# Output projection of an encoder layer: sixteen plain blocks, or one level of Strassen's form under a list scheduler

## The chip, the cores and the metric

The kernel runs on one core of a Trainium2 chip. The core has five engines that run side by side, each in the order of its own queue, and wait for one another through semaphores: PE (TensorE, matmuls into PSUM), DVE (VectorE), ACT (ScalarE), POOL (GpSimd) and SP (SyncE). DMAs are issued from SP's queue and from POOL's. The metric is the device time of one execution in microseconds (us). Three runs of the kernel before gave 1225.41, 1226.53 and 1227.11, median 1226.53.

## The reference

One encoder layer for 1024 tokens (`S`) of width 1024 (`D`), in float32:

```python
h = rmsnorm(x, norm1_g) * (1.0 + sc1) + sh1          # sh, sc, gt: from silu(c) @ w_ada + b_ada
z = h @ w_in                                         # u, v, q, k, va, gate_a, gate_b
a_out = gmlp_branch(u, v, gm_v_g, gm_w_s, gm_b_s) @ w_a
b_out = window_attention_branch(q, k, va, q_norm_g, k_norm_g, attn_sink) @ w_b
merged = jax.nn.sigmoid(gate_a) * a_out + jax.nn.sigmoid(gate_b) * b_out
x = x + gt1 * (merged @ w_o)                         # the output projection
h2 = rmsnorm(x, norm2_g) * (1.0 + sc2) + sh2
f_gate, f_up = jnp.split(h2 @ w_ffn_in, 2, axis=-1)
x = x + gt2 * ((jax.nn.silu(f_gate) * f_up) @ w_ffn_out)
```

The change concerns `merged @ w_o`, a product of 1024 x 1024 by 1024 x 1024, with the residual, the factor `gt1` and the sums of squares for the second norm.

## The kernel before, in words

Activations lie transposed: features on the 128 partitions, tokens along the free axis, in two token halves A and B of 512 (`HALF`). A float32 operand is split into a high part (rounded to fp32r, a cast on ACT) and a low part (the difference, a subtraction on DVE); a product is three matmuls, high by high, high by low and low by high (`mm3`, L161; `multiply`, L1286, for Strassen blocks). One matmul has a 128 x 128 stationary block and 512 moving columns. Nearly all operations are recorded under L79, the line of a small wrapper that can pin instructions to program order (`in_order`); loads are L131, stores L134.

The layer runs in this order.

- `half(0)` and `half(1)` (L568): for each token half the norm, the q and k projections, attention and gMLP. Attention is a loop of eight steps (four blocks of 128 tokens, two key/value heads; the `for s in range(nw)` loop). A step forms scores on PE, adds the bias and takes the maximum on DVE, takes exponentials on ACT (`exps`, which begins with a tiny DVE addition into `es`), normalises on DVE (`normalise`: sum, reciprocal, four products on the tiles `lb`), and in the next step transposes the tiles on PE. `fill` puts other matmuls (the u projection, two gate blocks) between. After the last step the transposes follow after two `fill` groups. Weight units are loaded by SP into a ring of three `raw` tiles, cast by ACT, and their low part in this loop is made by POOL.
- `ada_late` is one column block of the adaLN modulation: a DVE dot product of a 128 x 1024 weight tile with silu(c). 24 such blocks are worked off in the queue `ada_queue`: 4 at the end of `half(0)`, 12 in `half(1)`, and 8 in the output projection of half A, for which `cond` (silu(c)) is loaded again.
- `gate_products` (L1295): six of the eight 128-feature groups of the gates, already in one level of Strassen's form (Winograd's variant): the two token halves and the two halves of the contraction make 2 x 2 blocks, and seven products (`STEPS`) replace eight. Its results are the tiles `merged[half]`.
- `out_projection(hf, m, m_next)` (L1395), once for each half: for each of eight output groups `d`, eight contraction blocks of three matmuls (24 matmuls) into one PSUM bank, then on DVE `x1 = bank * gt1 + x`, the square on ACT and its addition on DVE, and a store of the rows to DRAM (`x1d`) on POOL's queue. A weight unit of w_o (128 x 1024) is prepared two groups ahead, so w_o is read twice. During half A the high and low parts of half B's `merged` are made, and the eight adaLN blocks. During half B the second norm of half A runs (`second_norm`, reading `x1d` back), and six units of the FFN's weights are made or loaded (`first_unit`, `early`, `raw2`). The order is that of the framework's scheduler, apart from the places that are pinned.
- The FFN, under `manual_schedule` (every engine's instructions in the order in which the code issues them): the first product pair of the gate, with `col_rstd` (column sums of half B's squares on PE) after the second product and `spread` (the reciprocal root, spread over partitions by PE) after the third; then seven products for each feature group, and the output product in the same form.

Tiles live in rings: `mid` has 8 tiles of 128 x 2048, `h` 4, `raw`, `wh` and `wl` (weights and their parts) 3 each, the PSUM banks `mm` and `at` 4 each. A new tile of a ring waits until an earlier one has been used for the last time.

Of the kernel before, what the change touches and what calls it, by code (L numbers as in the profile page):

```python
# [37 lines left out]
BIAS = 4  # L38


@with_exitstack
def kernel(
# [86 lines left out]

    def load(dst, src):  # L130
        tc.keep_in_program_order(nc.sync.dma_start(dst, src))  # L131
# [116 lines left out]
    tB = dram.tile([NP, P, 4 * HALF], F32, tag="tB", name="tB")  # L248

# [252 lines left out]
    def open_ffn():  # L502

        apool_ctx.close()
        fp = ffn_ctx.enter_context(pool("ffn"))
        fps.append(fp)
        for part in range(2):
            t = fp.tile([P, 2048], F32R, tag=f"b22{'hl'[part]}", name=nm("first"))
            firsts[part] = t

    def first_unit(i):

        r = raw_unit(w_gate[EARLY - 2 + i])
        h, l = (firsts[p][:, i * UNIT : (i + 1) * UNIT] for p in range(2))
        A.copy(h, r)
        V.tensor_tensor(l, r, h.bitcast(F32), op=ALU.subtract)
        return h, l
# [50 lines left out]
    def half(hf):  # L568
# [417 lines left out]
        pts = None  # L986
        for s in range(nw):
            if s:
# [3 lines left out]
                den = exps(*sc, work[s][1])  # L992
            fill(FA)
# [301 lines left out]
    def gate_products(hH, hL):  # L1295
# [21 lines left out]
        for d in GD:  # L1317
            banks = {}
            for i, (u, part, t, b, first) in enumerate(STEPS):
# [30 lines left out]
                elif i == 6:  # L1350
# [3 lines left out]
                    if d == KT - 1:  # L1354
                        split(merged[0][1][:, 3, :], mH[1][:, 3, :], mL[1][:, 3, :])
                    gate_low(d + 1, 1)
                run_tokens((0, 4, 4, 4, 0, 0, 0)[i])
                if d == KT - 1:
# [6 lines left out]
                    if i == 4:  # L1365
                        wo_units.append(unit(w_o[0]))
                    if i == 6:
                        wo_units.append(unit(w_o[1]))
# [21 lines left out]
        in_order[0] = False  # L1390
        return (mH, mL), merged[1]

    wo_units = []

    def out_projection(hf, m, m_next):  # L1395

        mH, mL = m
        if hf == 1:
            h2[0] = [[hid(), hid()], [hid(), hid()]]
            dst = h2[0]  # L1400
            x1B.extend([midt(F32, 4), midt(F32, 4)])
            h2m.extend([midt(F32, 4), midt(F32, 4)])
        else:
            out = [[midt(F32R, 4), midt(F32R, 4)] for _ in range(2)]
            cond = midt(F32, 2)[:, 0, :]
            load(cond, cd)
        ss = ss_tile()[:, :HALF]

        def second_norm(k):
            xk = stream("hs")  # L1410
# [4 lines left out]
        for d in range(KT):  # L1415
# [8 lines left out]
            if hf == 1 and d == 6:  # L1424
                early.append(unit(w_gate[0], V))
# [573 lines left out]
```

## Time and profile before

| | us |
|---|---|
| median of three runs | 1226.53 |
| span of the profiled execution | 1224.2 |
| PE busy | 1217.5 |
| PE weight loads busy | 1016.0 |
| DVE busy | 897.4 |
| ACT busy | 578.5 |
| POOL busy | 148.7 |

The profiled execution's own span, from its first instruction to its last, is 1224.2 us, 2.3 below the median of the runs, which also hold what lies around the span. An engine's busy time is the union of its instructions' records; matmul records overlap their successors, so the time of one matmul is read from start to start. A row of a timeline gives the start, the time from the first start to the last end, the engine, the line, the operation, the tile written and those read, and how many instructions are merged; in brackets stands the idle time before it and what ended it. The mean granted clock of PE was 1.000.

### The profile page before, as it was taken

Reading aid. Unit: us, or ns where it says so; the run is one execution under the profiler, and the core shown is the slowest. Engines: PE = TensorE matmul, PEld = TensorE weight load, DVE = VectorE, ACT = ScalarE, POOL = GpSimd, SP = SyncE. Lnnn points to the kernel's source line nnn. Section 1 sums busy time; section 2 is a strip of 40 time slices with the busy share of each in tenths; the row PEclk is TensorE's granted clock in tenths of the full one; section 3 lists DMA queues with packets and bytes.
Section 4 is the critical chain, followed back from the end, with each engine's and each line's share of the span. In section 5 each row is a group of like instructions: output and inputs, shape, how many; then the busy total and the mean of one; then the engine's idle time right before and its main releaser. Section 6 shows DMA issues by size and latency. Waiting matters only on the chain.

```text
span 1224.2 us, 15630 instructions
## 1 busy us (share of the span) xinstructions
PE 1217.5 (99%) x5701; PEld 1016.0 (83%) x5701; DVE 897.4 (73%) x1449; ACT 578.5 (47%) x944; POOL 148.7 (12%) x178
## 2 busy tenths in 40 slices
PE   9999999999999999999999999999999999999998
PEld 7888888888888888888888888888888888888887
DVE  9988877788878766877797766675676766765646
ACT  5667855367855434634453233333333334433341
POOL 0124323114331000011000001000000000010001
PEclk9999999999999999999999999999999999999999
DMA  9721179521176333597413446455555439995552
GB/s 366 283 86 52 35 241 361 223 86 53 35 276 222 120 104 121 198 322 264 154 52 120 172 155 224 172 176 202 189 189 187 167 153 367 393 364 190 189 172 104
DMA packets 75937, 230.79 MB, mean 189 GB/s; under 512 B 8658, under 2 KB 8914, under 8 KB 71124
## 3 DMA queue, kind: packets, MB, share of 16 engines
q1 hardware_dynamic: 61444, 161.62, 38.3%
q0 software_dynamic: 14416, 68.17, 14.9%
q8 instruction: 45, 0.74, 0.3%
q14 instruction: 32, 0.26, 0.1%
HBM read 174.70 MB, written 55.05 MB: 188 GB/s over the span
## 4 chain that ended last, share of the span: by engine, by line
PE 92%; DMA 4%; DVE 2%; issue 1%; ACT 1%; SPq 0%; POOL 0%; POOLq 0%; DVEq 0%; ACTq 0%
PE mm L79 48%; PE at L79 45%; DMA wS<-wo 1%; DMA mid<-in_w_ada_dram 1%; DMA raw<-in_w_q_dram 1%; DMA wo<-in_w_out_dram 1%; DMA mid<-in_xA_dram 0%; DVE mid L79 0%; ACT mid L79 0%; DVE wl L79 0%; DVE ws L79 0%; ACT wh L79 0%; DVE lb L79 0%; DVE hid L79 0%; DVE wo L79 0%
## 5 line engine op out<-in xcount | busy, mean ns | idle before, releaser
L79 PE MATMUL mm<-mid,wh 128*128 128x512 f32 x704 | 217.4, 390 | 0.0
L79 ACT CAST wh<-raw 128x1024 fp32r<-128x1024 f32 (+1 forms) x151 | 154.3, 1023 | 120.9 <-PE mm L79 45.6
L79 DVE TENSOR_TENSOR wl<-raw,wh 128x1024 fp32r<-128x1024 f32 (+1 forms) x137 | 161.5, 1183 | 62.1 <-ACT wh L79 61.1
L79 PEld LDWEIGHTS mm<-mid,wh 128*128 128x128 f32 x704 | 131.7, 188 | 27.1
L79 PE MATMUL mm<-mid,wl 128*128 128x512 f32 x352 | 137.0, 389 | 0.0
L79 PE MATMUL mm<-wh,h 128*128 128x512 f32 x384 | 124.6, 396 | 0.2 <-ACT h L79 0.2
L79 PE MATMUL mm<-h,wh 128*128 128x512 f32 x400 | 123.9, 391 | 0.0
L79 PEld LDWEIGHTS mm<-h,wh 128*128 128x128 f32 x400 | 74.6, 188 | 15.4
L79 PE MATMUL at<-h,wh 128*128 128x512 f32 x272 | 84.0, 390 | 0.0
L79 PEld LDWEIGHTS mm<-wh,h 128*128 128x128 f32 x384 | 70.8, 188 | 13.8 <-ACT h L79 0.4
L79 DVE TENSOR_TENSOR wl<-ws,wh 128x1024 fp32r<-128x1024 f32 (+1 forms) x54 | 60.7, 1125 | 24.5 <-ACT wh L79 24.5
L79 PE MATMUL mm<-h,wl 128*128 128x512 f32 x200 | 77.9, 389 | 0.0
L79 PEld LDWEIGHTS mm<-mid,wl 128*128 128x128 f32 x352 | 66.1, 188 | 13.8
L79 ACT CAST wh<-ws 128x1024 fp32r<-128x1024 f32 (+1 forms) x54 | 52.5, 973 | 42.3 <-DVE ws L79 27.4
L79 PE MATMUL mm<-wl,h 128*128 128x512 f32 x192 | 71.2, 391 | 0.0
L79 ACT ACTIVATE t<-t 128x512 f32<-128x512 f32 x53 | 32.8, 630 | 72.0 <-DVE t L79 71.9
L79 PEld LDWEIGHTS at<-h,wh 128*128 128x128 f32 x272 | 50.9, 188 | 10.5
L79 DVE TENSOR_TENSOR ol<-raw,oh 128x1024 fp32r<-128x1024 f32 x30 | 36.5, 1223 | 30.0 <-ACT oh L79 28.4
L79 ACT ACTIVATE xs<-xs 128x512 f32<-128x512 f32 x21 | 13.3, 633 | 94.0 <-DVE xs L79 94.0
L79 PE MATMUL at<-h,wl 128*128 128x512 f32 x136 | 53.1, 390 | 0.3 <-DVE wl L79 0.3
L79 PE MATMUL at<-wl,wh 128*128 128x512 f32 (+1 forms) x136 | 52.7, 388 | 0.0
L79 PE MATMUL at<-wh 128*128 128x512 f32 (+1 forms) x136 | 52.7, 387 | 0.0
(275 smaller groups left out, 2729.5 us busy)
## 6 DMA issues: line engine op xcount, KB each, us to landing
raw<-in_w_gate_dram SPq DMA_DIRECT2D x28, 512.0 KB, 3.8
tA<-hid POOLq DMA_DIRECT2D x11, 1024.0 KB, 4.6
tB<-hid POOLq DMA_DIRECT2D x11, 1024.0 KB, 5.0
wo<-in_w_out_dram POOLq DMA_DIRECT2D x22, 512.0 KB, 5.9
wS<-wo POOLq DMA_DIRECT2D x11, 1024.0 KB, 5.2
raw<-wS SPq DMA_DIRECT2D x44, 256.0 KB, 3.5
raw<-tB SPq DMA_DIRECT2D x44, 256.0 KB, 4.8
mid<-in_w_ada_dram SPq DMA_DIRECT2D x20, 512.0 KB, 9.8
```

Of the source, the lines that this page charges most:

```text
L79: ins = f(*args, **kw)
```

## The change

The output projection of both halves becomes one call, `out_products(merged)`, under `manual_schedule`. With A and B the token halves and the two halves of the contraction as blocks, four pairs of output groups (`p`, an even and an odd group) each take seven products of twelve matmuls: M1 and M2 for the even group of half A; T2, T3 and T4 accumulate onto M1's bank; T1 and B22 share another bank. 28 products take the place of sixteen groups of 24 matmuls, 336 matmuls of 384.

- The blocks T1 to T4 are sums of the `merged` tiles. The first sum (half A minus half B) is made for four tiles in `gate_products`, the others in `blocks()`, all on DVE, with the high part on ACT and the low part on DVE.
- Sums of w_o's blocks come out of `merged_sums`: in the attention loop of `half(1)` SP loads two units of w_o in every second step, DVE makes four sums, and POOL stores them to a new DRAM tensor `sO`, from which the projection loads them. The instructions stand between `exps` and `normalise`; the last step has four sums.
- The eight adaLN blocks move to the attention loop of `half(0)`, at the same place, one for each step from the second on and two in the last. The load of `cond` in the projection goes.
- Each product's bank is read by one DVE accumulation straight into the residual rows, scaled by `gt1` or its negative: 28 instead of 16. The even rows of half A are stored after M2 and loaded again for the norm; the other rows of x are loaded into tiles that the blocks have freed (`new_rows`). The second norm of half A is made in place on these rows after the product T1 of the second pair.
- The order of all of it, on PE, DVE, ACT, POOL and SP, comes from `Plan`: every operation is added with an engine, a cost and names that it reads and writes; PE's and SP's operations keep the order in which they were added; the others are picked by a simulated start and, among those that could start within 0.3 us, by the latest start that their users allow.
- The tiles of the FFN's first weights and of its T2 and B22 blocks change places (`tt2`, `b22`), and `unit(w_o[2])` is made one product earlier in `gate_products` in the place of `w_o[1]`.

The diff, cut:

```diff
+class Plan:
+    COST = {"v512": 0.6, "v1024": 1.14, "p512": 0.66, "a512": 0.52, "a1024": 0.95, "small": 0.2,
+            "load": 0.4, "mm": 2.72, "few": 0.45, "pow": 1.5}
+    WAIT = {"V": 0.08, "A": 0.08, "T": 0.4, "D": 3.4, "G": 0.1}
+    def __init__(self):
+        self.ops, self.last, self.users = [], {}, {}
+    def add(self, eng, cost, fn, reads=(), writes=()):
+        n = len(self.ops)
+        deps = set()
+        for r in reads:
+            if r in self.last:
+                deps.add(self.last[r])
+        for w in writes:
+            deps.update(self.users.get(w, ()))
+            if w in self.last:
+                deps.add(self.last[w])
+        for r in reads:
+            self.users.setdefault(r, []).append(n)
+        for w in writes:
+            self.last[w], self.users[w] = n, []
+        self.ops.append((eng, self.COST[cost], fn, deps))
+    def order(self, free):
+        n = len(self.ops)
+        late = [1e9] * n
+        t = 0.0
+        for i, (eng, cost, _, _) in enumerate(self.ops):
+            if eng == "T":
+                late[i] = t
+                t += cost
+        for i in reversed(range(n)):
+            eng, cost, _, deps = self.ops[i]
+            for j in deps:
+                e, c = self.ops[j][:2]
+                late[j] = min(late[j], late[i] - c - self.WAIT[e])
+        queues = {e: [i for i in range(n) if self.ops[i][0] == e] for e in "VATDG"}
+        now = {e: free.get(e, 0.0) for e in queues}
+        done, start = {}, {}
+        while len(start) < n:
+            best = None
+            for e, q in queues.items():
+                for i in q[:1] if e in "TD" else q:
+                    deps = self.ops[i][3]
+                    if all(j in done for j in deps):
+                        at = max([now[e]] + [done[j] for j in deps])
+                        key = (max(at, now[e] + 0.3), late[i], i)
+                        if best is None or key < best[0]:
+                            best = (key, e, i, at)
+            _, e, i, at = best
+            queues[e].remove(i)
+            start[i] = at
+            now[e] = at + self.ops[i][1]
+            done[i] = now[e] + self.WAIT[e]
+        return sorted(range(n), key=lambda i: (start[i], i))
+    def run(self, free):
+        for i in self.order(free):
+            if self.ops[i][2] is not None:
+                self.ops[i][2]()
...
+    def merged_sums(p):
+        t = mid.tile([P, 2048], F32, tag="mid", name=nm("wo"))
+        for i in range(2):
+            load(t[:, i * UNIT : (i + 1) * UNIT], w_o[2 * p + i])
+        a11, a12, a21, a22 = (t[:, i * HALF : (i + 1) * HALF] for i in range(4))
+        ops = [(a22, a21, a22), (a21, a11, a21), (a11, a22, a11), (a12, a11, a12)]
+        def one(n):
+            out, a, b = ops[n]
+            V.tensor_tensor(out, a, b, op=ALU.add)
+            if n == 3:
+                store(sO[p], t)
+        return one
...
+            if hf == 0:
+                if s % 2 == 0:
+                    ada_load()
+                if s:
+                    ada_late(*ada_loaded.pop(0), silu_c)
+                if s == nw - 1:
+                    ada_late(*ada_loaded.pop(0), silu_c)
+            else:
+                if s % 2 == 0:
+                    pair_sums.append(merged_sums(s // 2))
+                if s:
+                    for n in range(2):
+                        pair_sums[(s - 1) // 2](2 * ((s - 1) % 2) + n)
+                if s == nw - 1:
+                    for n in range(2):
+                        pair_sums[-1](2 + n)
...
+                if d in (4, 5) and i in (1, 3):
+                    k = 2 * (d - 4) + i // 2
+                    o = merged[1][0][:, k, :]
+                    V.tensor_tensor(o, merged[0][0][:, k, :], o, op=ALU.subtract)
...
+                    if i == 5:
+                        wo_units.append(unit(w_o[2]))
...
-    def out_projection(hf, m, m_next):
...
+    def out_products(merged):
+        (m0, m1), (x0, x1) = merged
+        NPAIR = KT // 2
+        T1 = oblk["T1"]
+        T2 = oblk["T2"] = (fpt("tt2h"), fpt("tt2l"))
+        B22 = oblk["B22"] = (fpt("b22h"), fpt("b22l"))
+        T3 = oblk["T3"] = (midt(F32R, 4), midt(F32R, 4))
+        T4 = oblk["T4"] = (midt(F32R, 4), midt(F32R, 4))
...
+        def blocks():
+            high("B21", m1, "m1", 3)
+            lo("B21", m1, "m1", 3)
+            for k in KS:
+                high("T1", x0, "x0", k)
+                lo("T1", x0, "x0", k)
+            for k in KS:
+                add("V", "v512", lambda k=k: negsum(x0[:, k, :], x1[:, k, :], x0[:, k, :]),
+                    [f"x1{k}"], [f"x0{k}"])
+                high("T2", x0, "x0", k)
+                lo("T2", x0, "x0", k)
+            for m, mn, name in ((m0, "m0", "T3"), (m1, "m1", "T4")):
+                for k in KS:
+                    add("V", "v512", lambda k=k, m=m: negsum(m[:, k, :], x0[:, k, :], m[:, k, :]),
+                        [f"x0{k}"], [f"{mn}{k}"])
+                    high(name, m, mn, k)
+                    lo(name, m, mn, k)
+            for k in KS:
+                high("B22", x1, "x1", k)
+                lo("B22", x1, "x1", k)
...
+        def fetch(key, parts):
+            r = f"raw{count['raw'] % 3}"
+            count["raw"] += 1
+            def go():
+                tiles[key] = wpool.tile([P, UNIT], F32, tag="raw", name=nm("raw"))
+                for cs, src in parts:
+                    load(tiles[key][:, cs], src)
+            add("D", "load", go, [], [r])
+            return r
+        def make(key, parts, to=None):
+            r = fetch(key, parts)
+            w = to
+            if to is None:
+                w = f"w{count['w'] % 3}"
+                count["w"] += 1
+            def hi():
+                if key not in units:
+                    units[key] = wtiles()
+                A.copy(units[key][0], tiles[key])
+            add("A", "a1024", hi, [r], [w + "h"])
+            add("V", "v1024", lambda: split_low(tiles[key], *units[key]), [r, w + "h"], [w + "l"])
+            names[key] = w
...
+        def need(kind, p):
+            if kind == "0":
+                make((kind, p), [(all_, w_o[2 * p])])
+            elif kind == "B":
+                make((kind, p), [(cs, w_o[2 * (p + i) + 1][:, HALF:]) for i, cs in enumerate((lo_, hi_))])
+            else:
+                i = "AC".index(kind)
+                make((kind, p), [(cs, sO[p][:, (2 * j + i) * HALF : (2 * j + i + 1) * HALF])
+                                 for j, cs in enumerate((lo_, hi_))])
...
+        USE = {"M1": ("0", 0, "B11", "a", True), "M2": ("0", 1, "B21", "b", True),
+               "T2": ("A", 0, "T2", "a", False), "T3": ("A", 1, "T3", "a", False),
+               "T4": ("B", None, "T4", "a", False), "T1": ("C", 1, "T1", "c", True),
+               "B22": ("C", 0, "B22", "c", False)}
...
+        def accumulate(get, tn, p, b, sc, d):
+            def go():
+                t = get()
+                V.scalar_tensor_tensor(out=t, in0=banks[p, b], scalar=sc[:, d : d + 1], in1=t,
+                                       op0=ALU.mult, op1=ALU.add)
+            add("V", "p512", go, [f"{'b' if b == 'b' else 'a'}{p}"], [tn])
...
+        need("0", 2)
+        c11 = [stream(("xs", "hs")[p % 2]) for p in range(NPAIR)]
+        for p in range(NPAIR):
+            add("D", "load", lambda p=p: load(c11[p], x_rows(0, 2 * p)), [], [f"c{p}"])
...
+        def new_rows(hf, q, old):
+            def go():
+                if hf == 0 and q == 0:
+                    h2[0] = [[hid(), hid()], [hid(), hid()]]
+                (x1B if hf else h2m).append(midt(F32, 4))
+            add("D", "load", go, [], [f"{old}{k}" for k in KS] + [f"{'gh'[hf]}{d}" for d in range(4 * q, 4 * q + 4)])
+            for d in range(4 * q, 4 * q + 4):
+                if hf or d % 2:
+                    add("D", "load", lambda d=d: load(row(hf, d), x_rows(hf, d)), [], [rn(hf, d)])
+        def even_rows(q):
+            for d in (4 * q, 4 * q + 2):
+                add("D", "load", lambda d=d: load(row(0, d), x1d[d * P : (d + 1) * P, :HALF]),
+                    [f"x1d0{d}"], [rn(0, d)])
...
+        new_rows(1, 0, "x0")
+        new_rows(0, 0, "m0")
...
+        second = [(p, name) for q in (0, 2) for name in ("T2", "T3", "T4") for p in (q, q + 1)]
+        for n, (p, name) in enumerate(second):
+            product(p, name)
+            if n == 2:
+                need("A", 2)
+            elif n == 3:
+                need("A", 3)
+                new_rows(1, 1, "m1")
+            elif n == 5:
+                need("B", 2)
+                new_rows(0, 1, "x1")
+            elif n == 7:
+                add("D", "load", new_firsts, [], [f"T2{x}{k}" for x in "hl" for k in KS]
+                    + [f"f{i}{x}" for x in "hl" for i in range(2)])
+                make(("f", 0), [(all_, w_gate[EARLY - 2])], "f0")
+            elif n == 8:
+                even_rows(0)
+                need("C", 0)
+            elif n == 9:
+                make(("f", 1), [(all_, w_gate[EARLY - 1])], "f1")
+                need("C", 1)
+                even_rows(1)
+            elif n == 11:
+                need("C", 2)
+            d = 2 * p + (name != "T2")
+            hf = int(name != "T4")
+            accumulate(lambda hf=hf, d=d: row(hf, d), rn(hf, d), p, "a", gt if name == "T2" else ngt, d)
+            if name == "T4":
+                square(lambda d=d: row(0, d), rn(0, d), 0, d)
...
+        third = [(p, name) for q in (0, 2) for name in ("T1", "B22") for p in (q, q + 1)]
+        for n, (p, name) in enumerate(third):
+            product(p, name)
+            if n == 0:
+                add("T", "few", col_sums, ["ss"], ["pt"])
+                add("V", "small", root_ms, ["pt"], ["ms"])
+                add("G", "pow", root, ["ms"], ["rcol"])
+            elif n == 1:
+                add("T", "few", spread_out, ["rcol"], ["rb"])
+                for k in range(KT):
+                    add("V", "p512", lambda k=k: norm_scale(k), ["rb"], [rn(0, k)])
+                    add("A", "a512", lambda k=k: norm_high(k), [rn(0, k)], [f"hh{k}"])
+                    add("V", "v512", lambda k=k: norm_low(k), [rn(0, k), f"hh{k}"], [f"hl{k}"])
+            elif n == 2:
+                need("C", 3)
+            elif n == 3:
+                make(("g", 0), [(all_, w_gate[0])])
+            elif n == 6:
+                make(("g", 1), [(all_, w_gate[1])])
+                fetch(("g", 2), [(all_, w_gate[2])])
+            d = 2 * p + (name == "T1")
+            accumulate(lambda d=d: row(1, d), rn(1, d), p, "c", ngt if name == "T1" else gt, d)
+            square(lambda d=d: row(1, d), rn(1, d), 1, d)
...
+        plan.run({"V": 2.5, "A": 1.5, "T": 0.0})
...
+    merged = gate_products(*half(1))
+    in_order[0] = False
+    manual[0] = True
+    with tc.manual_schedule():
+        out_products(merged)
...
```

198 lines of the change are left out of this document (119 added, 79 removed).

## The prediction

> **What bounds the kernel now.** I read the page first (busy shares, then the chain that ended last), then a table of stages, then the timelines of PE, DVE and POOL around the stages that the diff touches.
>
> ```profile
> span 1224.2 us, 15630 instructions
> PE 1217.5 (99%) x5701; PEld 1016.0 (83%) x5701; DVE 897.4 (73%) x1449; ACT 578.5 (47%) x944; POOL 148.7 (12%) x178
> PE 92%; DMA 4%; DVE 2%; issue 1%; ACT 1%; SPq 0%; POOL 0%; POOLq 0%; DVEq 0%; ACTq 0%
> ```
>
> PE is busy for 1217.5 of 1224.2 us: only fewer matmuls can shorten the kernel, and any wait that PE is given lengthens it. The stage table (span, then busy time of PE, PEld, DVE, ACT, POOL, granted clock, DMA share, GB/s):
>
> ```profile
> 389.00:500.00 111.00, 111.00 (x491) 91.91 (x490) 78.18 (x108) 50.30 (x76) 0.00 (x0) 1.00 0.37 122
> 500.00:589.00 89.00, 89.00 (x402) 73.92 (x401) 69.00 (x95) 37.73 (x50) 9.58 (x16) 1.00 0.80 271
> 506.00:520.00 14.00, 14.00 (x63) 11.62 (x62) 13.29 (x19) 7.40 (x11) 1.64 (x3) 1.00 0.85 293
> 603.00:660.00 57.00, 57.00 (x252) 46.81 (x251) 51.50 (x76) 29.07 (x46) 0.59 (x1) 1.00 0.17 59
> ```
>
> The output projection (500 to 589) keeps PE full with DVE at 78%. DVE at 95% (506 to 520) and 90% (603 to 660, the start of the FFN) has also left PE without a gap. PE's rows, the first one from the chain in order of time:
>
> ```profile
> 388.74 2.72 PE at L79 x12
> 500.10 0.62 PE L79 MATMUL mm<-h,wh 128*128 128x512 f32 x2
> 549.06 0.95 PE L79 MATMUL at<-ones,ss 128*128 128x1 f32 x8
> 555.45 1.05 PE L79 MATMUL at<-ident,rcol 128*128 128x128 f32 x8
> 589.02 0.62 PE L79 MATMUL at<-h,wh 128*128 128x512 f32 x2
> ```
>
> A product of twelve matmuls takes 2.72 us, 0.2267 each. The projection runs from 500.10 to 589.02: 88.92 us = 384 x 0.2267 (87.04) + 1.88 for the column sums and the spread of the norm, 0.94 each. No gap.
>
> **The gain.** Seven quarter products instead of eight: 28 products of twelve, 336 matmuls. PE needs 28 x 2.72 + 1.88 = 78.0 us, which is 10.9 less. All of it is on the path.
>
> **DVE's bill in the new stage.** The start-to-start times of DVE's dense rows price its work:
>
> ```profile
> 508.80 2.49 DVE L79 TENSOR_TENSOR mid<-mid,mid 128x512 fp32r<-128x512 f32 x4
> 511.20 1.22 DVE L79 TENSOR_TENSOR wl<-raw,wh 128x1024 fp32r<-128x1024 f32 x1
> 512.34 0.68 DVE L79 TENSOR_TENSOR mid<-mid,mid 128x512 fp32r<-128x512 f32 x1
> 517.29 1.22 DVE L79 SCALAR_TENSOR_TENSOR raw<-raw,mid 128x1024 f32<-128x1024 f32 x1
> 518.43 0.08 DVE L79 DVE_READ_ACCUMULATOR raw<-raw,mid 128x1 f32 x1
> 557.69 0.74 DVE L79 SCALAR_TENSOR_TENSOR mid<-hs,mod,at 128x512 f32<-128x512 f32 x1
> 558.35 0.68 DVE L79 TENSOR_TENSOR ss<-ss,t 128x512 f32<-128x512 f32 x1
> ```
>
> 512 columns take 0.60 (2.40 for four), 1024 columns 1.14, an operation on PSUM 0.66. The plan holds 33 block sums and low parts (19.8), 16 low parts of weights (18.2), 28 accumulations out of PSUM (18.5), 14 adds of squares (8.4), 16 norm operations (10.6) and 0.3 of small ones: 75.8 us in 109 instructions. The eight adaLN dots (1.14 each) and the eight old low parts of the second half leave the stage. ACT's bill, 21 casts and 24 squares or norm parts of 512 and 16 casts of 1024 at the list's 0.52 and 0.95, is 39 us, half of the stage.
>
> What DVE has is less than the stage. The gate stage's tail comes first:
>
> ```profile
> 500.99 0.69 DVE L79 SCALAR_TENSOR_TENSOR t<-t,hs 128x512 f32<-128x512 f32 x1 [0.70 <-ACT t L79]
> 594.46 0.95 PE L79 MATMUL at<-ones,ss 128*128 128x1 f32 x8
> 595.44 0.16 DVE L79 TENSOR_SCALAR ms<-at 128x4 f32<-128x4 f32 x1 [1.41 <-PE at L79]
> 598.13 1.05 PE L79 MATMUL at<-ident,rcol 128*128 128x128 f32 x8
> ```
>
> From 500.99 four operations of 0.60 (two merges, two adds) keep DVE until about 503.4, 3.3 us after PE has begun; the list assumes 2.5. At the other end PE takes the squares of the second half two products into the FFN (in the row 5.44 after 589.02), in the new order at 500.1 + 78.0 + 5.44 = 583.5. Supply 80.1, demand 75.8: DVE may idle 4.3 us in all before PE waits. Three places, counted by what must be done when:
>
> 1. The rows of x for token half B come into tiles that the T blocks free. Before that stand one low part of B21, two of weights, T1's four, T2's sums and lows, T3's and T4's sums: 14.9 us, 518.3; the load lands 4 us later (row below), and the accumulation that needs it is due at 524.6. If the four M1 accumulations (2.6) go first, it just fails. T4 then starts at 532.7 with 27.7 us due of 29.3. At the 5% that DVE idled at its densest (0.71 of 14 us) the two places cost about 0.8.
> 2. The norm's column sums and spread are again one product apart, as at 594.46 and 598.13, where PE did not wait: 0.
> 3. After the spread (61.7 us into the stage) come 16 norm operations, seven accumulations, seven adds, two weights: 10.6 + 4.6 + 4.2 + 2.3 = 21.7 us, for 21.7 until 583.5. At 5% idle that is 1.1 short, and the low part of the next gate weight (1.14), behind it in the queue and due one product later, adds some 0.7: 1.8. Bounds: nothing (work done earlier), and 6 us (all 4.3 us of slack spent before, and 1.8).
>
> The list scheduler places loads by 3.4 us; measured, and what ACT waited for them:
>
> ```profile
> raw<-in_w_o_dram SPq DMA_DIRECT2D x16, 512.0 KB, 5.3
> xs<-in_xB_dram SPq DMA_DIRECT2D x8, 256.0 KB, 4.0
> ACT wh L79 <- DMA raw<-in_w_o_dram: 16.8, 6, 5.5
> ```
>
> SP issues 47 loads there instead of some 53 and the traffic falls from 24 MB to about 18, so I leave it at the figures above. The stores of x stay at sixteen on POOL's queue.
>
> **What moves into attention.** In token half A eight adaLN dots (eight 512 KB loads on SP), in half B sixteen sums of w_o (eight 512 KB loads on SP, four 1 MB stores on POOL) stand between the exponentials and the normalisation. There DVE waited anyway:
>
> ```profile
> 132.24 0.16 DVE L79 TENSOR_TENSOR den<-den,es 128x4 f32<-128x4 f32 x1 [1.39 <-ACT es L79]
> 136.94 2.41 POOL L79 TENSOR_TENSOR wl<-raw,wh 128x1024 fp32r<-128x1024 f32 x1
> 138.89 0.47 DVE L79 TENSOR_TENSOR es<-rows,nmx 128x4 f32<-128x4 f32 x1
> 140.56 0.16 DVE L79 TENSOR_TENSOR den<-den,es 128x4 f32<-128x4 f32 x1 [1.20 <-ACT es L79]
> 140.97 1.41 DVE L79 TENSOR_SCALAR lb<-lb,den 128x384 f32<-128x384 f32 x4
> 142.71 1.47 PE L79 MATMUL at<-ident,lb 128*128 128x128 f32 x12
> 321.49 1.14 DVE L79 TENSOR_TENSOR es<-rows,nmx 128x4 f32<-128x4 f32 x1
> 322.91 0.16 DVE L79 TENSOR_TENSOR den<-den,es 128x4 f32<-128x4 f32 x1 [0.27 <-ACT es L79]
> 323.32 1.14 DVE L79 TENSOR_SCALAR lb<-lb,den 128x256 f32<-128x256 f32 x4
> 324.83 1.03 PE L79 MATMUL at<-ident,lb 128*128 128x128 f32 x8
> 298.01 0.33 SPq L131 DMA_DIRECT2D raw<-in_w_s_dram  x1
> 329.97 1.06 ACT L79 CAST wh<-raw 128x1024 fp32r<-128x1024 f32 x1
> ```
>
> One dot (1.14 + 0.08) or two sums (1.20) fill a gap of 1.39: nothing in the second to seventh of the eight steps, where other matmuls stand between the products and their transposes. The last step takes a double portion and its transposes follow at once. Half A: two dots and the small sum end at 141.8, the four products with den 1.82 later at 143.6; the fourth transpose wanted the last of them at 143.0: PE waits 0.6. Half B: four sums from 322.63 to 325.03, products at 326.58, wanted at 325.1: 1.5. Together 2.1 (nothing, if the sums run while es waits; 4.8, the portions in full, if nothing covers them). SP runs ahead here (w_s is loaded at 298.01 and cast at 329.97), so the new loads are early too, and what is queued behind them has time; POOL, at 12% of the span, has room for four DMA issues, behind which its low parts wait. The four sums added to the gate stage (2.4 us) are hidden: DVE is busy 78 of its 111 us.
>
> DVE's es ends at 139.36, when POOL's low part ends (136.94 + 2.41 = 139.35). The Trainium skill, "SBUF — State Buffer", section "Who interferes with whom", says that a DVE instruction with two SBUF inputs and a GpSimd instruction that reads SBUF exclude each other for the whole instruction. The trace agrees, with es at 0.47 us here. By that rule a new operation that met POOL's 2.41 us unit would wait up to that long, and one such meeting at an unprotected place would add up to 2.4; but each stands behind an es that has already waited POOL out.
>
> **The sum.** -10.9 + 2.1 + 0.8 + 1.8 = -6.2. The profiled execution spans 1224.2 and the median is 1226.53, 2.3 outside the span, unchanged: 1220.3 us.
>
> **The rivals.** 0.2% is 2.45 us, about what this kernel's runs can tell from no change.
>
> A. Clean: list and gaps cover everything, 1226.5 - 10.9 = 1215.6. For it: no gap of PE at 90 and 95% of DVE. Against: the double portions and a DVE at 95% over 80 us.
>
> B. DVE becomes the bound. In a fixed order, 0.1 us lost at each of 109 instructions is 10.9; less the 4.3 of slack, PE waits 6.6 at the FFN's entry instead of 1.8: 1220.3 + 4.8 = 1225.1. For it: waits of 0.2 us on ACT are common in DVE's rows.
>
> C. Slower: SP's queue. Loads of x that wait for a freed block stand ahead of weight loads, and each T product needs the accumulation before it out of the same bank. There are four such reallocations; at 5.3 us a landing instead of 3.4, after a late block, each could hold PE 3.4 us: 13.6, which with attention's 2.1 ends at 1231.3. Slower from 13.3 us of waits on. For it: ACT's 16.8 us of waiting for w_o; against: those waits, up to 5.5 us, never reached PE.
>
> D. A wait long enough to cost clock.
>
> ```profile
> L79 PE MATMUL mm<-mid,wh 128*128 128x512 f32 x704 | 217.4, 390 | 0.0
> L79 PE MATMUL at<-zeros 128*128 128x512 f32 x10 | 4.2, 600 | 1.9 <-DVE identr L79 1.9
> ```
>
> After the idle start ten matmuls took 600 ns each, where 390 is usual. If B's one wait sends PE back to that, ten matmuls lose 0.21 each, 2.1 us: 1227.2. "TensorE: Matmul & The Clock Gate" of the Trainium skill, section "What's actually happening", puts this at half clock after an idle window of about 3.4 us; no granted clock below 1.00 in the stages quoted tests it.
>
> **How the numbers follow.** Forecast 0.50 (1217.5 to 1223.5), A 0.17, B 0.18, C 0.10, D 0.05. The range 1215.3 to 1226.6 leaves out C, most of D and the edges, below 0.2. Faster by over 0.2% (under 1224.1): forecast, A and just over half of B, 0.77; within: the rest of B and D, 0.13; slower: C, 0.10.
>
> **What would show it.** Right: about 5653 matmuls; 78 to 82 us from the first projection product to the FFN, DVE over 90% in it; a wait of PE for lb at the last attention step of each half; the next at the FFN's norm. Wrong: PE gaps at T products, DVE waiting on DMA; or attention steps longer than before in the middle of the loop.

## The result, and the profile after

The changed kernel takes 1233.0 us (median of four runs, 1232.2 to 1234.32) against 1226.57 for the kernel before in the same session: a ratio of 1.0056, 95% interval 1.0042 to 1.0071. It is slower by some 6.4 us; the forecast was 1220.3 and faster.

First the page of the changed kernel (span, then engines), which answers the first fence of the prediction, and PE's waits by what ended them (engine and tile, releaser, sum in us, times, longest).

```profile
span 1232.5 us, 15626 instructions
PE 1220.7 (99%) x5653; PEld 1006.7 (82%) x5653; DVE 928.6 (75%) x1504; ACT 582.6 (47%) x954; POOL 150.6 (12%) x182
```

```profile
PE mm L145 <- ACT h L145: 1.6, 2, 1.4
PE at L145 <- DVE lb L145: 1.4, 1, 1.4
PE at L145 <- DVE t L145: 1.3, 1, 1.3
```

The 48 matmuls are gone (5653 of 5701), but PE is busy for 3.2 us more than before. Of PE's waits, the first line's belongs almost whole to the start-up; the others were forecast in kind, and all are small (two more, of 0.8 and 0.7 in all, and the one of 1.9 at the very start, which the kernel before has too, are left out). A loss of 8 us of span with 48 matmuls fewer is more than they hold, so the matmuls themselves must have become slower. The rows of PE's timeline that mark the stages, first of the kernel before, then of the changed one (start, time, engine, tiles, count):

```profile
15.52 1.20 PE L79 MATMUL mm<-wh,h 128*128 128x512 f32 x4
...
388.58 0.62 PE L79 MATMUL at<-h,wh 128*128 128x512 f32 x2
...
1018.84 0.39 PE L79 MATMUL at<-oh 128*128 128x512 f32 x1
...
1220.09 0.28 PE L79 MATMUL mm<-wh,wl 128*128 128x256 f32 x1
```

```profile
17.11 1.20 PE L145 MATMUL mm<-wh,h 128*128 128x512 f32 x4 [1.39 <-ACT h L145]
...
328.75 1.56 PE L145 MATMUL at<-ident,lb 128*128 128x128 f32 x8 [1.36 <-DVE lb L145]
...
393.08 0.62 PE L145 MATMUL at<-h,wh 128*128 128x512 f32 x2
...
506.52 0.62 PE L145 MATMUL mm<-h,wh 128*128 128x512 f32 x2
...
586.70 0.63 PE L145 MATMUL at<-h,wh 128*128 128x512 f32 x2
...
603.68 0.73 PE L145 MATMUL at<-h,wh 128*128 128x512 f32 x2 [1.28 <-DVE t L145]
...
621.55 1.64 PE L145 MATMUL at<-h,first 128*128 128x512 f32 x6 [0.59 <-DVE mid L145]
...
1025.86 0.39 PE L145 MATMUL at<-oh 128*128 128x512 f32 x1
...
1228.10 0.28 PE L145 MATMUL mm<-wh,wl 128*128 128x256 f32 x1
```

With 500.10 and 589.02, which stand in the prediction, the differences give what each stage did. The last two columns are the kernel of the experiment e5 below, read at the same instructions. Four of its marks:

```profile
392.10 0.62 PE L145 MATMUL at<-h,wh 128*128 128x512 f32 x2
...
503.62 0.62 PE L145 MATMUL mm<-h,wh 128*128 128x512 f32 x2
...
583.55 0.62 PE L145 MATMUL at<-h,wh 128*128 128x512 f32 x2
...
1014.21 0.39 PE L145 MATMUL at<-oh 128*128 128x512 f32 x1
```

| stage, up to its last mark | before | after | gained (-) or lost | e5 | gained (-) or lost |
|---|---|---|---|---|---|
| start-up, to 15.52 | 15.52 | 17.11 | +1.59 | 16.53 | +1.01 |
| both token halves, to the gate | 388.58 | 393.08 | +2.91 | 392.10 | +2.51 |
| gate stage | 500.10 | 506.52 | +1.92 | 503.62 | 0.00 |
| output projection | 589.02 | 586.70 | -8.74 | 583.55 | -8.99 |
| FFN | 1018.84 | 1025.86 | +9.34 | 1014.21 | +0.84 |
| output product, to the last matmul | 1220.09 | 1228.10 | +0.99 | 1215.46 | 0.00 |

The projection delivers most of its gain. The gate stage, the FFN and the output product give it back, and the diff hardly touches the matmuls of these three. The start-up's 1.59 is not put down to the change: the code there is the same, and the first mark of the other kernels below lies from 0.17 before to 1.49 after that of the kernel before; the 1.49 is that of e7, the kernel before with 64 idle bytes.

How the loss looks: the chain of waits in order of time (start, duration, what), in the FFN, before and after.

```profile
656.63 2.72 PE mm L79 x12
...
662.07 5.44 PE mm L79 x24
...
705.59 38.08 PE at L79 x168
```

```profile
660.77 2.80 PE at L145 x12
663.58 5.56 PE mm L145 x24
...
708.09 38.72 PE at L145 x168
```

A product of twelve matmuls took 2.72 us, now 2.80 for some; fourteen products take 38.72 instead of 38.08. There is no gap in these pieces: PE is busy without a break and simply slower. 0.64 for two feature groups is 0.32 a group: 1.92 for the six of the gate stage, all that this stage lost, and 7.0 for the 22 of the FFN. The granted clock is 1.00 in these stages. The groups of instructions, kept apart by form (count, busy us, mean ns of one), tell which matmuls they are; before, then after:

```profile
L79 PE MATMUL mm<-h,wh 128*128 128x512 f32 x400 | 123.9, 391 | 0.0
...
L79 PE MATMUL at<-tt1h,wh 128*128 128x512 f32 x112 | 43.7, 390 | 0.0
```

```profile
L145 PE MATMUL mm<-h,wh 128*128 128x512 f32 x304 | 94.3, 391 | 0.0
...
L145 PE MATMUL at<-tt1h,wh 128*128 128x512 f32 x112 | 44.3, 395 | 0.0
```

Matmuls that stream the `h` tiles are as quick as before. Those that stream `tt1` take 5 ns longer (395 for 390), and `tt2` and `b22` do likewise. Their tiles lie in a memory pool behind all the small tiles, and the change adds a small tile that the shortened diff ahead of the prediction leaves out:

```diff
+        ngt = small.tile([P, KT], F32, tag="ngt1", name="ngt1", bufs=1)
+        V.tensor_scalar(ngt, mod[:, GT1 : GT1 + KT], -1.0, None, op0=ALU.mult)
```

It is 8 floats, 32 bytes a partition, for the negated gate column. By the lists of tile places in the built programs, the pool of the weights' parts `wh` and `wl` begins at byte 19776 of a partition, `h` and `mid` at 56640 and 89408, all 64 past a multiple of 128. So did the pool of the T blocks, at 175424; after the change it begins at 175456.

### The profile page after: what moved, and what is told of

The parts are those of the page before. It is cut to its first block, busy times and chain, and to the rows that moved or that the text cites. A ratio compares the mean times of both kernels' runs of the same rounds, so it can differ in the third digit from the quotient of the medians.

```text
span 1232.5 us, 15626 instructions
## 1 busy us (share of the span) xinstructions
PE 1220.7 (99%) x5653; PEld 1006.7 (82%) x5653; DVE 928.6 (75%) x1504; ACT 582.6 (47%) x954; POOL 150.6 (12%) x182
## 4 chain that ended last, share of the span: by engine, by line
PE 91%; DVE 4%; DMA 2%; ACT 2%; issue 1%; SPq 0%; ACTq 0%; DVEq 0%
PE mm L145 46%; PE at L145 45%; DVE mid L145 2%; DMA raw<-in_w_q_dram 1%; DMA ws<-in_w_up_dram 1%; DVE wl L145 0%; ACT lb L145 0%; DMA mid<-in_xA_dram 0%; ACT mid L145 0%; DVE lb L145 0%; ACT pH L145 0%; DVE wo L145 0%; DVE ss L145 0%; DVE pL L145 0%; DVE xs L145 0%
## 5 line engine op out<-in xcount | busy, mean ns | idle before, releaser
L145 PE MATMUL mm<-mid,wh 128*128 128x512 f32 x640 | 198.7, 391 | 0.7 <-DVE mid L145 0.7
L145 PEld LDWEIGHTS mm<-mid,wh 128*128 128x128 f32 x640 | 119.8, 188 | 26.8 <-DVE mid L145 1.1
L145 PE MATMUL mm<-mid,wl 128*128 128x512 f32 x320 | 124.9, 390 | 0.0
L145 PE MATMUL at<-h,wh 128*128 128x512 f32 x304 | 94.1, 391 | 1.3 <-DVE t L145 1.3
L145 PE MATMUL mm<-h,wh 128*128 128x512 f32 x304 | 94.3, 391 | 0.0
L145 PEld LDWEIGHTS mm<-mid,wl 128*128 128x128 f32 x320 | 60.0, 188 | 13.6
L145 PEld LDWEIGHTS at<-h,wh 128*128 128x128 f32 x304 | 56.8, 188 | 13.7 <-DVE t L145 2.1
L145 PEld LDWEIGHTS mm<-h,wh 128*128 128x128 f32 x304 | 56.6, 188 | 11.7
L145 PE MATMUL mm<-h,wl 128*128 128x512 f32 x152 | 59.3, 390 | 0.0
L145 PE MATMUL at<-h,wl 128*128 128x512 f32 x152 | 59.2, 389 | 0.0
```

Source lines behind the costliest of these rows:

```text
L145: ins = f(*args, **kw)
```

## The experiments

All are measured against the kernel before in the same session (1226.09, 1226.38 and 1226.73 us in the three sessions). "Pace" below is what the 512-column matmuls lost in all: the sum, over all their start-to-start times of 0.19 to 0.262 us, of the difference from 0.2267. It was 2.4 us for the kernel before and 13.7 for the changed one, 11.3 more.

**e1: the changed kernel with the new tile padded to 64 bytes.**

```diff
-        ngt = small.tile([P, KT], F32, tag="ngt1", name="ngt1", bufs=1)
+        ngt = small.tile([P, 2 * KT], F32, tag="ngt1", name="ngt1", bufs=1)[:, :KT]
```

> The changed kernel with one edit: the new small tile ngt1 takes 16 columns instead of 8, of which 8 are used, so that the tiles of the attention, FFN and output pools, which lie behind it, start on a multiple of 64 bytes again (in the changed kernel they start 32 bytes past one). Theory L, layout: products whose moving operand starts 32 bytes off take 2.80 us instead of 2.72. Seven products with three such operands took 19.36 us against 19.04 in the kernel before; that is 0.32 x 28 feature groups (9.0), 1.0 in the output product, 1.0 in the projection, some 0.3 in attention: 11.3 us go, and the time is 1221.7 us, 0.4% below the kernel before; every product is back at 2.72. Rival W, work: the slower products come from DVE and DMA sharing the memory with PE, whose work grew; then nothing changes: 1233 us, products at 2.80.

Measured: 1230.32 us, ratio 1.0033 (1.0021 to 1.0046); pace 9.4 instead of 13.7. The interval of the ratio just meets the changed kernel's, so it is the pace that shows that the place matters; a multiple of 64 doesn't restore it. The groups of e1, by form:

```profile
L145 PE MATMUL at<-tt1h,wh 128*128 128x512 f32 x112 | 44.2, 394 | 0.0
...
L145 PE MATMUL at<-tt1l,wh 128*128 128x512 f32 x112 | 43.5, 388 | 0.0
```

One matmul of the three is back (388), another is not (394), and the third, left out here, takes 392; by the chain of waits a product takes 2.76:

```profile
653.19 2.76 PE mm L145 x12
```

**e2: the kernel before, with 32 idle bytes among its small tiles, and nothing else.**

```diff
+    shift = small.tile([P, 8], F32, tag="shift", name="shift", bufs=1)
+    V.memset(shift, 0.0)
```

> The kernel before with one edit: an extra tile of 32 bytes per partition, written once, in the pool of small tiles, so that the same pools start 32 bytes later; no other work. Theory L: 0.32 x 28 groups (9.0) + 1.0 in the output product + 0.3: 10.3 us more, 1236.8 us, with 2.80 us for the products on T1, T2 and B22. Rival W: no change, 1226.5 us.

Measured: 1235.73 us, ratio 1.0079 (1.0064 to 1.0095), 9.6 us slower, pace 12.7; the chain of waits has the changed kernel's pieces:

```profile
661.95 2.80 PE at L79 x12
...
709.26 38.72 PE at L79 x168
```

So the loss needs none of the change's work. Thirty-two bytes that nobody reads cost more than the change's whole balance.

**e3 and e4: two waits, each alone, on top of e1.** In e3 the double portion of the last attention step goes behind that step; in e4 the FFN's first two up weights are asked for before the next gate weight.

```diff
-                if s == nw - 1:
-                    ada_late(*ada_loaded.pop(0), silu_c)
...
-                if s == nw - 1:
-                    for n in range(2):
-                        pair_sums[-1](2 + n)
...
+        if hf == 0:
+            ada_late(*ada_loaded.pop(0), silu_c)
+        else:
+            for n in range(2):
+                pair_sums[-1](2 + n)
```

```diff
-        load_gate(0)
         load_up(0)
         load_up(1)
+        load_gate(0)
```

> e1_align, and the second portion of the last attention step (one adaLN dot in token half A, two sums of w_o in half B) moved behind the last value products, just before the gMLP products, where DVE waited for PE. Theory: the portion in the last step held up the transposes of the normalised tiles by 0.7 us in half A and 1.4 to 2.2 in half B; without it the two waits go, 2.1 to 2.9 us less than e1_align. Rival: the wait only moves, to the products of gMLP or the copies behind them; then within 0.5 us of e1_align.

> e1_align, and at the start of the FFN the two loads of w_up are issued before the load of the gate's unit 0, which must wait for a free raw tile. Theory: in the changed kernel DVE idled 2.45 us until the first w_up tile landed, and PE then 1.28 us for DVE's chain; with the loads ahead both go: 1.3 us less than e1_align. Rival: DVE's backlog alone holds PE there, and the wait stays or comes back one product later: within 0.4 us of e1_align.

Measured: e3 1229.01 us (ratio 1.0026, 1.0017 to 1.0035), e4 1228.3 (1.0014, 1.0006 to 1.0023), against 1.0033 for e1. The intervals overlap, so the times alone don't prove either gain; the waits do show what happened. A line of PE's waits in e3, then one of e1 that e4 doesn't have:

```profile
PE mm L145 <- DVE wl L145: 1.7, 1, 1.7
```

```profile
PE at L145 <- DVE t L145: 1.0, 1, 1.0
```

In e3 the wait for `lb` is gone, but a new one of 1.7 for a weight's low part stands in its place. In e4 the wait of 1.0 for `t` at the FFN's entry is gone, and no other took its place. That wait is no fixed price, though: e3 and e5, which keep the old order of loads, have 0.2 of it and none.

**e5: the changed kernel with no tile added**, the negated column in a part of an older tile that is dead by then.

```diff
-        ngt = small.tile([P, KT], F32, tag="ngt1", name="ngt1", bufs=1)
+        ngt = acc_mod[:, GT1 : GT1 + KT]
```

> The changed kernel with no tile added: the negated gate column is written into eight columns of an older tile that are dead by then, so that every later pool begins where it began before the change (175424). If the pool's place is what slows the matmuls (layout theory): every product of the gate and FFN stages back at 2.72 us, seven products at 19.04 instead of 19.36, the output products at 208.8 instead of 209.8, and the time at 1221 to 1222.5, which is 10 to 12 below the changed kernel and 4 to 5.5 below the kernel before. If it is the change's added work on VectorE and GpSimd that disturbs the matmuls (work theory): 1231 to 1233 as the changed kernel.

Measured: 1223.31 us, ratio 0.9968 (0.9956 to 0.9981), pace 2.5. The change, without its 32 bytes, is 9.7 us quicker than with them and faster than the kernel before. By the page of e5, PE's busy time falls by 7.9 against the kernel before:

```profile
PE 1209.6 (99%) x5653; PEld 1007.6 (83%) x5653; DVE 928.4 (76%) x1504; ACT 582.6 (48%) x954; POOL 150.8 (12%) x182
```

And its chain of waits is back at the old pieces:

```profile
663.17 2.72 PE at L145 x12
...
701.25 38.08 PE at L145 x168
```

**e6 and e7: is it the address, or the distance between two addresses?** The kernel before with 32 (e6) or 64 bytes (e7) ahead of everything, so that all pools move together.

```diff
+    shift = const.tile([P, 8], F32, tag="shift", name="shift")     # e7: [P, 16]
+    V.memset(shift, 0.0)
     ident = const.tile([P, P], F32, tag="ident", name="ident")
```

> The kernel before with 32 bytes put ahead of everything, so that every pool with matmul operands (weights, hidden, T blocks) moves by 32 bytes together. If what counts is each address by itself against multiples of 64 (absolute theory): all the products are slow, also those that stayed at 2.72 us with the later pools alone moved, so more than the 9.6 us lost there: 1236 to 1262. If what counts is how the pools stand to each other (relative theory): no change, 1224 to 1228.5, products at 2.72.

> The kernel before with 64 bytes put ahead of everything: all pools at a multiple of 128, where they had been 64 past one. With the later pools alone there (first experiment), the products on them took 2.755 us against 2.72. Absolute theory (128 is what counts, at 64 past): the products on all pools at 2.75 or more, 1230 to 1245. Absolute theory with 64 as the grain, and relative theory: no change, 1224 to 1228.5. With the run that moves everything by 32 this parts three cases.

Measured: 1226.54 us (ratio 1.0002, 0.9993 to 1.0011; pace 2.4) and 1226.35 (0.9999, 0.999 to 1.0008; pace 2.5). Nothing changes: neither the bytes nor the added instruction cost anything by themselves. What counts is how the pools stand to one another.

**e9: the weights alone out of step.** The kernel before, the pool of `raw`, `wh` and `wl` moved by 32 bytes and all others by 128.

```diff
+    padp = ctx.enter_context(pool("padp"))
     hpool = ctx.enter_context(pool("hpool", 4))
...
+    shift = const.tile([P, 8], F32, tag="shift", name="shift")
+    V.memset(shift, 0.0)
+    pad = padp.tile([P, 24], F32, tag="pad", name="pad")
+    V.memset(pad, 0.0)
```

> The kernel before with the pool of split weights alone moved by 32 bytes against 128; every other pool with matmul operands moves by 128. If what slows a matmul is how its weights stand to its moving operand, then every 512-column matmul with one operand among the weights and the other elsewhere is slow, in all stages, not only those on the T blocks: the trace of before has 3,840 of them, and at the 0.0067 us measured on the T blocks (0.2333 against 0.2267) that is 25.7, so 1252; 1239 if 96 bytes cost half of what 32 cost. If it is the later pools' place against something else (the hidden pool, the T blocks of the other pool, their neighbours), no change: 1224 to 1228.5, since all of those still stand as before to each other.

Measured: 1249.84 us, ratio 1.0189 (1.0174 to 1.0205), 23.1 us slower than 1226.73; pace 27.3. Every matmul that pairs a weight with a tile of another pool is slow, the `h` ones too, while a product with both operands among the weights (`at<-wh`) is not. The groups of e9, by form:

```profile
L79 PE MATMUL mm<-h,wh 128*128 128x512 f32 x400 | 125.9, 396 | 0.0
...
L79 PE MATMUL at<-wh 128*128 128x512 f32 x134 | 52.1, 389 | 0.0
L79 PE MATMUL at<-tt1l,wh 128*128 128x512 f32 x112 | 44.6, 398 | 0.0
```

That settles which relation: the pool of the weights against those of the tiles that are multiplied with them. 25.7 was expected from 3,840 matmuls at 0.0067; the pace grew by 24.9.

**e10: the later pools out of step by 96 bytes** (e2 with a tile of 24 floats).

```diff
+    shift = small.tile([P, 24], F32, tag="shift", name="shift", bufs=1)
```

> The kernel before with the later pools (T blocks, output) moved by 96 bytes, where 32 cost 9.6 us and 64 cost about a third of the pace. If the cost goes by the distance to the nearest multiple of 128 (96 is 32 below one): 1235 to 1236.5 as with 32. If it grows or falls with the distance itself: 96 is worse than 64 (1236 and more), or better than it (1226.5 to 1229). No change would say that only some of the 32-byte steps count.

Measured: 1237.16 us, ratio 1.0088 (1.0074 to 1.0102), 10.4 us slower, pace 14.0, much as with 32 bytes. Its chain of waits:

```profile
653.93 2.81 PE mm L79 x12
```

Summed up, by the distance of the moving tiles' pool from the weights' (its remainder by 128), and the products that it concerns. The 128 is not shown to be the period: by the lists of tile places, the two operands of each matmul that the pace counts begin a multiple of 512 bytes apart in the kernel before, and no run tried a distance of 128, 256 or 384.

| kernel | distance in bytes | moving tiles concerned | pace, us | time against before |
|---|---|---|---|---|
| before, e6, e7 | 0 | | 2.4 to 2.5 | +0.2 and 0.0 |
| e5 | 0 | | 2.5 | -3.1, the change's gain |
| e2 | 32 | T blocks | 12.7 | +9.6 |
| e10 | 96 | T blocks | 14.0 | +10.4 |
| e9 | 96 | all with operands in two pools | 27.3 | +23.1 |
| after | 32 | T blocks | 13.7 | +6.4, the change's gain in it |
| e1 | 64 | T blocks | 9.4 | +4.2, the change's gain in it |

e1 and the changed kernel stand 7.0 and 9.7 us above e5, which differs from them in this alone.

**e8 and e11: can the rest be had?** e8 is e5 with the edits of e3 and e4. In e11 the two adds of half B that e3 moved go to GpSimd instead, behind the normalisation of the last step.

```diff
             normalise(sc[0], sc[2], den)
...
             if s == nw - 1:
+                if hf == 1:
+                    for n in range(2):
+                        pair_sums[-1](2 + n, G)
```

> The changed kernel in the old layout, with the two moves that were tried one by one: the double portion of the last attention step handed to after the step (a cost of 1.3 us less was measured) and the two up weights asked for before the gate weight at the FFN's entry (2.0 less was measured). Layout theory and both moves adding up: 1230.3 of the aligned one goes to 1221.5 without the layout's rest, less 1.3 and 2.0, so 1217.5 to 1219.5, some 0.6 per cent below the kernel before. If the moves only shift the waits once the matmuls are quick: 1220 to 1222.

> The fastest so far (1221.4) had one new wait of PE, 1.43 us on a weight's low part in half B's gMLP, where VectorE was busy without a break behind the two adds that had been moved there. Here GpSimd makes these two adds in the last attention step of half B, behind the normalisation. If VectorE's queue was the cause, the wait falls to under 0.5 and the time to 1219.8 to 1220.8. If GpSimd's adds hold VectorE's short operations up there (es and den waited for GpSimd's weight part in the changed kernel), the wait comes back ahead of the probabilities' transposes: 1221 to 1223.

Measured: e8 1221.4 us (ratio 0.9961, 0.9947 to 0.9974), e11 1221.63 (0.9963, 0.995 to 0.9975). Both beat the kernel before and the changed one; against e5's 0.9968 neither is told apart. The attention wait was not won, it was moved. In e8 PE's row for `lb` no longer waits, and 42 us later PE waits 1.43 for a weight's low part; in e11 that wait is 0.3 and the one for `lb` is back, because VectorE's four products were held up. PE in e8 (two rows), then VectorE in e8, VectorE in e11 and POOL in e11:

```profile
326.27 1.56 PE L145 MATMUL at<-ident,lb 128*128 128x128 f32 x8
...
368.12 0.50 PE L145 MATMUL mm<-mid,wl 128*128 128x512 f32 x1 [1.43 <-DVE wl L145]
```

```profile
325.87 1.14 DVE L145 TENSOR_SCALAR lb<-lb,den 128x256 f32<-128x256 f32 x4
```

```profile
326.26 3.05 DVE L145 TENSOR_SCALAR lb<-lb,den 128x256 f32<-128x256 f32 x4
```

```profile
326.02 2.62 POOL L145 TENSOR_TENSOR wo<-wo 128x512 f32<-128x512 f32 x2 [1.43 <-DVE den L145]
```

Four products took 3.05 us instead of 1.14 while GpSimd's adds ran (326.02 to 328.64). By the Trainium skill, "SBUF — State Buffer", section "Who interferes with whom", a `tensor_scalar` in a two-port mode and a GpSimd instruction shut each other out; the trace agrees in its times, though which mode ran no row shows.

## Why the prediction was wrong, step by step

**The step that failed is the sum.** It took -10.9, 2.1, 0.8 and 1.8 and let every other stage stand as before; "a product of twelve matmuls takes 2.72 us" was read off one stage and kept for all. No term stood for the places of the tiles. In the changed kernel that term is 9.7 us in time (e5 against after) and 11.3 in pace: 0.3 in the token halves, 1.92 in the gate stage, 0.9 in the projection, 7.2 of the FFN's 9.34, 0.99 in the output product. Nothing in the profile before shows where a tile lies, but the new tile was there to be seen in the whole diff; its size alone would not have told the price.

**Rivals.** None of the four was it. B: VectorE did not become the bound; the projection took 80.18 us, and PE waited 1.87 at the FFN's entry instead of B's 6.6. C named 1231.3, near what came out, for another reason: no product waited 3.4 us for a freed block. D: the granted clock was 1.00 in all these stages. That C's number came near was luck, and would have misled a reader who had looked at the time alone.

**The gain.** Right in kind: 5653 matmuls, and a shorter projection. In size it fell short: -8.74 (-8.99 in e5) against -10.9 + 0.8 = -10.1.

**DVE's bill in the new stage.** 78.8 us was forecast (78.0 + 0.8), and 78 to 82 as what would show it right; it is 80.18, and 79.93 in e5. VectorE's share in the stage table of the changed kernel (span, then busy time of PE, PEld, DVE) is 93%, 76.35 of 82:

```profile
504.00:586.00 82.00, 81.32 (x361) 66.10 (x360) 76.35 (x108) 44.46 (x65) 8.67 (x15) 1.00 0.65 215
```

PE's timeline in the changed kernel has one wait worth the name there:

```profile
534.95 0.73 PE L145 MATMUL mm<-mid,wh 128*128 128x512 f32 x2 [0.68 <-DVE mid L145]
```

Place 1, the first T products, cost a wait of 0.68 here, and 0.34 and 0.82 in e5. By start-to-start times these pieces lose 1.0 and 1.5, so 0.8 was too low. Place 2, the norm, is right: no wait there.

**Place 3, the FFN's entry.** 1.8 was forecast; the two waits are 1.28 and 0.59, together 1.87. That the size came out is in part luck, for the first wait ends a chain from a load. VectorE in the changed kernel:

```profile
600.22 0.69 DVE L145 TENSOR_TENSOR ws<-ws 128x512 f32<-128x512 f32 x1 [2.45 <-DMA ws<-in_w_up_dram]
```

The sums of `w_up` stood in front of the norm's last work and waited for a transfer that SP had issued late. In e4, with the load asked for earlier, VectorE doesn't wait for it, nor PE for `t`. In e5, with the old order, VectorE waits 0.33 for it and PE not at all for `t`; there, where the pace is right, the whole FFN loses 0.84.

**Attention.** 0.6 and 1.5 were forecast. Half A: the twelve transposes that took 1.47 take 2.10, 0.63 more. Half B was mis-sized: the four sums lasted 2.86 (325.16 to 328.02) instead of the 2.40 reckoned, behind an `es` that ended 325.24, and the products began at 328.34. VectorE in the changed kernel:

```profile
324.09 1.15 DVE L145 TENSOR_TENSOR es<-rows,nmx 128x4 f32<-128x4 f32 x1
325.16 2.86 DVE L145 TENSOR_TENSOR wo<-wo 128x512 f32<-128x512 f32 x4
327.94 0.15 DVE L145 TENSOR_TENSOR den<-den,es 128x4 f32<-128x4 f32 x1
...
328.34 1.15 DVE L145 TENSOR_SCALAR lb<-lb,den 128x256 f32<-128x256 f32 x4
```

`den` follows at 327.94, 2.78 after the sums begin, so a sum costs 0.70 and not 0.60. PE's mark moves by 3.92, of which 1.59 is the start-up and 0.63 half A; the 1.70 left and the transposes' 1.56 instead of 1.03 make 2.2. As forecast, nothing is lost in the steps before the last.

With the layout restored, the steps add up to -8.99 + 2.51 + 0.84 = -5.64 in e5's trace, against the forecast -6.2. Its start-up takes 1.01 of that back in this execution, so the last matmul comes 4.63 earlier. This execution, at 1221.69, is quicker than e5's median; the medians are 3.1 apart, half of the forecast, by the interval of the ratio 2.3 to 5.4.

## What to carry to other kernels

Before a profile's price for a matmul is used for a changed kernel, ask whether the change adds, removes or resizes any tile that lies ahead of a matmul operand; a small tile can cost more than the work that it serves. Put small new tiles into dead parts of old ones, or pad so that all pools with matmul operands move by the same number of bytes, as in e6 and e7. After a change, compare the start-to-start time of the same product in stages that the change does not touch: a stage that is slower without a gap points to operands, not to order.

## What the runs showed of the hardware that was not expected

- A matmul's pace depends on where its weights lie against its moving operand. Where the distance leaves a remainder of 0 by 128 bytes (and by 512), twelve 512-column matmuls take 2.72 us; at 32, 2.80; at 96, 2.81 (e10); at 64, 2.76 (e1). It is the relation that counts: e6 and e7 move both and cost nothing, e9 puts the weights alone out of step and costs 23.1 us. By the Trainium skill, "SBUF — State Buffer", section "Who interferes with whom", the moving operand and the weight load read through two independent ports, and PE never waits on anyone. The runs differ from that: apart from one or two small memsets no other engine's work was changed in e2, e9 and e10, and the pace was. The measurement decides; by what mechanism the place of one operand comes to matter to the other, no run shows.
- The slowdown outlasts its cause by a few matmuls. In the changed kernel a product on a `mid` tile, which had not moved, begins with start-to-start times of 224 to 241 ns when it follows a product on a moved tile, and is back at 227 after seven matmuls. The output product shows it without any moved pairing: there each matmul has both operands in one pool (`oh` and `ol` in the moved one, `wh` and `wl` in that of the weights), and the 0.99 us is lost at the 30 changes between the two. The last matmul before a change takes 235 ns, the first seven after it 224 to 236. So the place of a neighbour's operands counts too; why, no run shows.
- It shows in no wait, in no granted clock and in no share of busy time: PE's is 99% in all these kernels, and 100% in e9, the slowest.
